# Loading the weight matrix by rows over all partitions instead of by quadrants

## The chip, the cores and the metric

The kernel runs on one core of one Trainium2 chip. The metric is the device time of one execution in microseconds (us); a time of a kernel is the median of several runs. The core has five engines that run their own instruction streams: PE (TensorE, matmul; PEld is its weight load), DVE (VectorE), ACT (ScalarE), POOL (GpSimd) and SP (SyncE, which here only issues transfers). Transfers run on the core's 16 DMA engines. SP, ACT and POOL each have a queue of their own for the transfers they issue.

## The reference

```
B, S, D = 16, 2048, 1024            # x: [B, S, D], w: [D, D], decay: [D], all float32
xw = x @ w
out[:, 0, :] = xw[:, 0, :]
for t in range(1, S):
    out[:, t, :] = decay * out[:, t - 1, :] + xw[:, t, :]
```

A matrix product, followed along time by a decayed running sum for each of the 1024 output channels.

## The kernel before

**Tiling.** Time is cut into 64 chunks of 512 steps (16 batches, 4 chunks each), and two chunks make a group. The 1024 output channels make 8 blocks of 128. A slot is one group and one block: PE sums 8 matmuls (k = 0 to 7, 128 input channels each) for each of the two chunks in PSUM, ACT, POOL and DVE run the decayed sum over it, DVE turns the result back (32x32 transposes), and SP stores it. The 1024 input channels are spread so that quadrant q of the partitions (32 partitions) holds channels 256q to 256q + 255, eight to a partition.

**The weights.** `wsb` holds w in bf16, ready for PE. It is filled from a staging area `stage[h, e]` in four quarters: h picks the left or right 512 columns, e the even or the odd rows. A quarter is 512 rows of 512 floats (1 MB). In the staging area a partition has four of them, m = 0 to 3, 512 columns each. `load_w(queues, h, e)` (L297) loads a quarter with four transfers. `settle(h, e, m, copy)` (L304, its copy is L306) casts or copies piece m of all 128 partitions into `wsb`, where it becomes the weights of k = 2m + e.

- Quarter (0, 0) is loaded at the very start, as float32, by SP and ACT in turn (the call just below `touch`). The first two transfers are SP's first and ACT's first, the others their second.
- The other three are cast to bf16 on the way by POOL's queue: (0, 1) between the first x pieces, (1, 0) and (1, 1) after the second chunk of x.

**The prologue's order is written out by hand.** The string `agenda[-99]` is carried out from left to right, and each engine keeps that order. The letters that matter: `M` loads half a chunk of x (POOL, L105, four transfers, one for each quadrant), `U` loads a w quarter on POOL's queue, `w` and `W` settle one piece on ACT or on DVE, `K` copies one element of an x quadrant into a gate (ACT, L341) and lets PE run dummy matmuls that read the gate (L324), `E` turns a piece of x (DVE, L115), `F` and `G` sort it for PE (L123).

```
-99: "M0 U0 M1 M2 M3 U1 U2 w0 W1 w2 W3 K0 K1 K2 K3 E0 E1 G0 E2 G1 E3 F2 G3 W4 w5 W6 W7 D E4 ..."
```

Ahead of it PE gets 22 dummy matmuls (`spin(22, ...)`) with nothing to wait for but a cleared tile. SP also issues four small loads of decay (L331), behind its two of w. A transfer that reuses a completion semaphore waits on its queue for the transfer that had it before; POOL has eight of them.

**The matmuls.** In slots 0 to 3 PE works through the first chunk in two pieces: for each piece first the even k (the quarter with e = 0), then the odd ones (e = 1). The right half (h = 1) is first used in slot 4. After that PE goes on slot by slot to the end, where the last four blocks are turned by PE itself and stored.

Of the kernel before, what the change touches and what calls it, by code (L numbers as in the profile page):

```python
# [14 lines left out]
def _ap(ap_obj: bass.AP, new_ap, extra_offset=0):  # L15
    return dataclasses.replace(
        ap_obj,
        ap=[list(p) for p in new_ap],
        offset=ap_obj.offset + extra_offset,
    )  # L20
# [5 lines left out]
def kernel(  # L26
# [27 lines left out]
    pin = tc.keep_in_program_order  # L54
    B, S, D = x.shape
    assert w.shape == (D, D)

    NQ = 4
    P = 32
    CQ = D // NQ  # L60
    K = CQ // P
    M = K // 2
# [4 lines left out]
    CH = D // 2  # L67
# [12 lines left out]
    def quad(q):  # L80
        return slice(q * P, (q + 1) * P)
# [184 lines left out]
    class Outlet:  # L266
# [8 lines left out]
        def store(self, b, t0):  # L275
# [4 lines left out]
            for j in range(0, self.nj, nj):  # L280
# [11 lines left out]
    stage = {(0, 0): room[0][:, 0:size],  # L292
             (0, 1): room[0][:, size:size * 3 // 2].bitcast(BF16),
             (1, 0): room[1][:, 0:size // 2].bitcast(BF16),
             (1, 1): room[1][:, size // 2:size].bitcast(BF16)}

    def load_w(queues, h, e):  # L297
        for i, q in enumerate((0, 2, 1, 3)):
            pin(queues[i % len(queues)].dma_start(  # L299
                out=stage[h, e][quad(q)].rearrange("p (m d) -> p m d", m=M),  # L300
                in_=_ap(w, [[2 * D, P], [2 * P * D, M], [1, CH]],
                        (q * CQ + e) * D + h * CH)))

    def settle(h, e, m, copy):  # L304
        src = stage[h, e][:, m * CH:(m + 1) * CH]
# [5 lines left out]
    rows = const.tile([128, 2, P], FP32, name="rows")  # L311
    touch = const.tile([128, 1], BF16, name="touch")
    load_w((nc.sync, nc.scalar), 0, 0)
    pin(nc.vector.memset(idle, 0.0))  # L314
    pin(nc.vector.memset(rows, 0.0))
# [14 lines left out]
    for q in range(NQ):  # L330
        pin(nc.sync.dma_start(  # L331
            out=rows[q * P:q * P + R],
            in_=_ap(decay, [[P, R], [CH, 2], [1, P]], q * CR)))
# [10 lines left out]
    def load_part(i):  # L344
        load_w((nc.gpsimd,), *((0, 1), (1, 0), (1, 1))[i])
# [292 lines left out]
```

## Time and profile before

| | us |
|---|---|
| median of 3 runs (904.95 to 906.10) | 905.39 |
| the profiled execution | 905.14 |
| its span, first to last instruction | 903.4 |
| time outside the span | 1.7 |
| PE busy in the span | 897.1 |
| DVE / ACT / POOL busy | 826.1 / 685.7 / 656.8 |
| first real matmul starts (L131) | 11.19 |
| first cast of w starts (L306, ACT) | 7.18 |

The span is what the profile sees of one execution; the time outside it belongs to the metric as well. Busy shares are means over the whole span. In a timeline line the first number is the start from the span's beginning, the second the length, then engine, line of the kernel, operation, output <- inputs, shape and count; several equal instructions that follow closely are one line. The bracket is the time that the engine sat idle before it, and what ended that. Where the profile lists DMA issues, the last number is the median time from issue to landing.

### The profile page before, as it was taken

How to read it: one execution, taken by the hardware profiler on the slowest of the kernel's cores; microseconds unless marked ns; L12 is line 12 of the kernel's file. 1: busy time of each engine (PE TensorE's matmuls, PEld its weight loads, DVE VectorE, ACT ScalarE, POOL GpSimd, SP SyncE). 2: the span in 40 equal slices, each digit the busy share in tenths (PEclk: the TensorE clock that was granted, in tenths of full speed). 3: DMA queues.
4: the chain of work that ended last, by engine and by line, in shares of the span. 5: the costliest groups of instructions: out<-in, count | busy, mean ns of one | idle time of the engine just before them, and what ended most of it. 6: DMA issues, size and time to landing. Idle time of an engine off the chain costs nothing.

```text
span 903.4 us, 12112 instructions
## 1 busy us (share of the span) xinstructions
PE 897.1 (99%) x4217; PEld 412.9 (46%) x4217; DVE 826.1 (91%) x628; ACT 685.7 (76%) x955; POOL 656.8 (73%) x755
## 2 busy tenths in 40 slices
PE   9999999999999999999999999999999999999997
PEld 6444444444444444444444444444444444444444
DVE  4999998999999999999998999999999999999997
ACT  4889867777877877877778778778777787787742
POOL 7988678777767768677677677777777776776632
PEclk9999999999999999999999999999999999999999
DMA  9999999999999999999999999999999999999868
GB/s 191 195 215 216 232 239 215 215 238 244 245 246 255 236 250 251 240 250 244 221 238 227 222 232 229 229 227 227 232 227 226 235 230 223 227 232 210 175 143 237
DMA packets 402542, 204.77 MB, mean 227 GB/s; under 512 B 8752, under 2 KB 401456, under 8 KB 402480
## 3 DMA queue, kind: packets, MB, share of 16 engines
q1 hardware_dynamic: 265168, 134.76, 61.0%
q0 software_dynamic: 137024, 68.70, 56.9%
q8 instruction: 33, 0.54, 0.2%
q10 hardware_dynamic: 288, 0.52, 0.2%
q14 instruction: 29, 0.24, 0.1%
HBM read 138.42 MB, written 134.22 MB: 302 GB/s over the span
## 4 chain that ended last, share of the span: by engine, by line
PE 95%; DMA 2%; POOL 1%; DVE 1%; issue 0%; ACT 0%; DVEq 0%; POOLq 0%
PE ps L131 94%; DMA xb<-in_x_dram 2%; POOL xb L105 1%; DMA ot<-in_w_dram 1%; PE spare L131 1%; DVE xw L115 0%; ACT xt L123 0%; DVE so L201 0%; DVE ot L258 0%; PE spare L388 0%; ACT xs L183 0%; PE ps L388 0%; DVE h L392 0%; ACT h L169 0%; POOL ot L299 0%
## 5 line engine op out<-in xcount | busy, mean ns | idle before, releaser
L131 PE MATMUL ps<-xt,wsb 128*128 128x512 bf16 (+2 forms) x4036 | 868.2, 378 | 0.2 <-ACT h L169 0.2
L131 PEld LDWEIGHTS <-wsb 128*128 128x128 bf16 x4168 | 407.4, 98 | 477.9 <-ACT wsb L306 0.8
L196 POOL TENSOR_TENSOR xs<-h,xs 128x512 f32<-128x512 f32 (+1 forms) x190 | 242.8, 1278 | 189.9 <-ACT h L169 85.0
L183 ACT COPY xs<-ps 128x1024 f32<-128x1024 f32 (+1 forms) x190 | 189.3, 996 | 156.2 <-PE ps L131 151.6
L258 DVE STREAM_TRANSPOSE ot<-so 128x1024 f32<-128x1024 f32 (+1 forms) x260 | 300.1, 1192 | 2.0 <-POOL so L190 1.1
L246 POOL TENSOR_TENSOR so<-h,xs 128x512 f32<-128x512 f32 (+1 forms) x190 | 241.2, 1271 | 42.6 <-ACT h L169 27.8
L123 ACT COPY xt<-xw 128x2048 bf16<-128x2048 bf16 (+3 forms) x136 | 242.2, 1790 | 7.7 <-DVE xw L115 7.7
L105 POOL DMA_DIRECT2D xb<-in_x_dram x264 | 174.2, 661 | 5.3 <-DMA xb<-in_x_dram 2.4
L169 ACT ACTIVATE h<-so,dec 128x512 f32<-128x512 f32 (+1 forms) x190 | 145.3, 766 | 27.1 <-DVE so L201 23.9
L115 DVE STREAM_TRANSPOSE xw<-xb 128x2048 f32<-128x2048 f32 (+3 forms) x78 | 147.4, 1901 | 6.3 <-DMA xb<-in_x_dram 6.3
L201 DVE TENSOR_TENSOR_SCAN so<-spare,keep,xs 128x512 f32<-128x512 f32 (+1 forms) x97 | 120.0, 1240 | 27.4 <-POOL xs L196 27.1
L201 DVE TENSOR_TENSOR_SCAN so<-spare,xs 128x512 f32<-128x512 f32 x93 | 113.3, 1220 | 27.4 <-POOL xs L196 24.5
L169 ACT ACTIVATE h<-ps,dec 128x512 f32<-128x512 f32 (+1 forms) x190 | 130.1, 685 | 0.0
L221 DVE TENSOR_TENSOR_SCAN so<-dec,ps 128x1024 f32<-128x1024 f32 x34 | 76.8, 2261 | 1.0 <-ACT h L169 1.0
L221 DVE TENSOR_TENSOR_SCAN so<-dec,keep,ps 128x1024 f32<-128x1024 f32 (+1 forms) x35 | 76.0, 2171 | 0.2 <-issue 0.2
L250 ACT COPY keep<-so 128x1 f32<-128x1 f32 x136 | 25.4, 189 | 9.5 <-DVE so L221 9.0
L192 ACT COPY so<-keep 128x1 f32<-128x1 f32 x97 | 18.5, 191 | 2.5 <-DVE ot L258 2.3
L131 PE MATMUL ps<-xw,wsb 128*128 128x256 bf16 (+3 forms) x68 | 11.2, 301 | 0.0
L190 POOL MEMSET so<- 128x1 f32 x93 | 10.7, 117 | 0.6 <-DVE ot L258 0.6
L131 PE MATMUL spare<-xt,wsb 128*128 128x512 bf16 (+3 forms) x52 | 10.7, 322 | 0.0
L324 PE MATMUL spare<-idle 128*128 128x512 bf16 x22 | 7.8, 536 | 1.2 <-DVE idle L314 1.2
L299 POOL DMA_DIRECT2D ot<-in_w_dram x12 | 6.5, 546 | 0.9 <-issue 0.4
(37 smaller groups left out, 37.2 us busy)
## 6 DMA issues: line engine op xcount, KB each, us to landing
out_dram<-ot SPq DMA_DIRECT2D x248, 512.0 KB, 10.9
xb<-in_x_dram POOLq DMA_DIRECT2D x248, 256.0 KB, 7.8
out_dram<-ot SPq DMA_DIRECT2D x12, 256.0 KB, 4.3
ot<-in_w_dram POOLq DMA_DIRECT2D x12, 128.0 KB, 5.8
xb<-in_x_dram POOLq DMA_DIRECT2D x8, 128.0 KB, 4.6
out_dram<-xb SPq DMA_DIRECT2D x3, 256.0 KB
xb<-in_x_dram POOLq DMA_DIRECT2D x4, 144.0 KB, 6.7
ot<-in_w_dram ACTq DMA_DIRECT2D x2, 256.0 KB, 5.1
```

What stands on the lines that cost most here:

```text
L105: pin(nc.gpsimd.dma_start(out=xb_of[c][quad(q), j0:j1], in_=_ap(x, [[D, P], [P * D, j1 - j0], [1, CQ]], (b * S + t0 + j0 * P) * D + q * CQ)))
L115: pin(nc.vector.transpose(out=dst.rearrange("p (m j i) -> p j m i", m=M, i=P)[:, j0:j1, m0:m1], in_=src.rearrange("p (j m c) -> p j m c", ...
L123: pin(copy(out=xt_of[c][:, m0:m1, :, j0 * P:j1 * P], in_=src))
L131: pin(nc.tensor.matmul(out=ps[:, t0:t1] if ps.shape[1] >= t1 else ps, lhsT=lhs, rhs=rhs, start=(k == 0 and t0 == start), stop=(stop and k ...
L169: pin(nc.scalar.activation(out=h, in_=src, func=mybir.ActivationFunctionType.Copy, scale=dec[:, self.n:self.n + 1]))
L183: pin(nc.scalar.copy(out=self.xs, in_=self.ps))
L196: pin(nc.gpsimd.tensor_tensor(out=odds, in0=self.g, in1=odds, op=ALU.add))
L201: pin(nc.vector.tensor_tensor_scan(out=so[:, 3:T + 2:2], data0=squares[-1][:, n:n + 1].to_broadcast([128, T // 2]), data1=self.xs[:, 1:T:2 ...
L221: pin(nc.vector.tensor_tensor_scan(out=so[:, t + 2:t + 2 + size], data0=dec[:, n:n + 1].to_broadcast([128, size]), data1=ps, initial=befor ...
L246: pin(nc.gpsimd.tensor_tensor(out=self.so[:, 2:T + 2:2], in0=self.h, in1=self.xs[:, 0:T:2], op=ALU.add))
L250: pin(nc.scalar.copy(out=self.keep, in_=self.so[:, self.T + 1:self.T + 2]))
L258: pin(nc.vector.transpose(out=outlet.ot[:, :, c0:c0 + P], in_=self.so[:, 2 + t0:2 + t0 + nj * P].rearrange("p (i t) -> p i t", t=P)))
```

## The change

Only `load_w` changes. Before, transfer i of a quarter fills one quadrant: 32 partitions, each with its four rows m = 0 to 3. After, transfer m fills one piece: row m of every one of the 128 partitions, in the columns m·512 to m·512 + 511 of the staging area. The bytes, the number of transfers, the queues and the place of the issues stay. The source pattern of a transfer was [32 partitions, 4 rows, 512 columns] and becomes [4 quadrants, 32 partitions, 512 columns]; the destination was 32 x 4 x 512 and becomes 128 x 512.

```diff
     def load_w(queues, h, e):
-        for i, q in enumerate((0, 2, 1, 3)):
-            pin(queues[i % len(queues)].dma_start(
-                out=stage[h, e][quad(q)].rearrange("p (m d) -> p m d", m=M),
-                in_=_ap(w, [[2 * D, P], [2 * P * D, M], [1, CH]],
-                        (q * CQ + e) * D + h * CH)))
+        for m in range(M):
+            pin(queues[m % len(queues)].dma_start(
+                out=stage[h, e][:, m * CH:(m + 1) * CH],
+                in_=_ap(w, [[CQ * D, NQ], [2 * D, P], [1, CH]],
+                        (2 * P * m + e) * D + h * CH)))
```

With it the waits change: before, a settle waited for all four transfers of its quarter, since each brings a part of every piece; after, a settle of piece m waits for transfer m alone. The order of the instructions on PE, DVE, ACT, POOL and SP is the same in both kernels. In the first quarter SP has m = 0 and 2, ACT has m = 1 and 3; of the settles, ACT has m = 0 and 2, DVE m = 1 and 3.

## The prediction

> **What bounds the kernel now.** I read the page first, then the timeline of the first 42 us, then the table of one-microsecond stretches, then the list of DMA issues, and last the end of the trace.
>
> ```profile
> span 903.4 us, 12112 instructions
> ...
> PE 897.1 (99%) x4217; PEld 412.9 (46%) x4217; DVE 826.1 (91%) x628; ACT 685.7 (76%) x955; POOL 656.8 (73%) x755
> ...
> PE 95%; DMA 2%; POOL 1%; DVE 1%; issue 0%; ACT 0%; DVEq 0%; POOLq 0%
> ```
>
> PE is busy for all but 6.3 us of the span, and 95% of the chain that ends last is PE. What happens once the first real matmul runs can hardly be shortened; a later first matmul moves everything behind it. The w loads stand only in the prologue, so the timeline of the prologue decides (start, duration, engine; in brackets the idle time before and what ended it):
>
> ```profile
> 0.74 0.90 ACTq L299 DMA_DIRECT2D ot<-in_w_dram  x2
> 0.75 0.86 SPq L299 DMA_DIRECT2D ot<-in_w_dram  x2
> ...
> 1.20 7.78 PE L324 MATMUL spare<-idle 128*128 128x512 bf16 x22 [1.20 <-DVE idle L314]
> ...
> 7.18 1.14 ACT L306 CAST wsb<-ot 128x512 bf16<-128x512 f32 x2 [4.02 <-DMA ot<-in_w_dram]
> ...
> 8.23 0.19 ACT L341 COPY gate<-xb 32x1 bf16<-32x1 bf16 x1
> ...
> 8.82 2.54 PE L324 MATMUL spare<-idle,gate 128*128 128x512 bf16 x11
> ...
> 11.19 0.55 PE L131 MATMUL ps<-xw,wsb 128*128 128x288 bf16 x3
> ```
>
> PE is never idle from 1.20 on: 22 dummy matmuls, then 11 that wait for the gate copies, then real work at 11.19. ACT makes the gate copies (K0 to K3 of the agenda) only after w0 and w2, its two casts of the first w quarter, and those wait 4.02 us for the loads. So a late w load holds up ACT, ACT the gates, and the gates PE. DVE likewise has W1 and W3 ahead of E0, the first transpose of x.
>
> **Step 1: how many DMA engines carry a load.** Bytes, number of loads (4 per quarter) and pieces (128 rows of 2 KB) stay the same. What changes is the shape. Before, both sides of a load begin with a dimension of 32. Changed, the source begins with 4 (the quadrants), the destination with 128 (the partitions). The kernel has one other load that begins with 4: decay.
>
> ```profile
> ot<-in_w_dram ACTq DMA_DIRECT2D x2, 256.0 KB, 5.1
> ot<-in_w_dram SPq DMA_DIRECT2D x2, 256.0 KB, 4.8
> ...
> rows<-in_decay_dram SPq DMA_DIRECT2D x4, 1.0 KB
> ```
>
> The w loads have a landing time behind their size, decay has none: this view gives one only when it finds sixteen completions for each transfer. In the trace's semaphore updates a w load counts sixteen while its data lands; the first decay load counts one at its issue, at 2.15, and four later. So a transfer that begins with 4 seems to be carried by four engines. The bounds for the new loads are 16 engines and 4; I take 4, the row that it is nearest to.
>
> [...]
>
> **Step 2: when the first quarter lands.** The stretches (PE, PEld, DVE, ACT, POOL busy, then clock, DMA share, GB/s):
>
> ```profile
> 2.00:3.00 1.00, 1.00 (x4) 0.42 (x3) 0.00 (x0) 0.99 (x2) 1.00 (x3) 1.00 0.91 258
> 3.00:4.00 1.00, 1.00 (x4) 0.33 (x3) 0.00 (x0) 0.16 (x1) 1.00 (x3) 1.00 0.98 332
> ...
> 12.00:13.00 1.00, 1.00 (x10) 0.75 (x9) 0.79 (x4) 1.00 (x2) 1.00 (x3) 1.00 1.45 194
> ```
>
> From 3 to 4 us only SP's and ACT's loads run: 332 GB/s over 16 engines is 20.8 GB/s each, 99 ns for a row of 2,048 B. The best slices in the DMA view of the first 3 us, 410 GB/s, give 80 ns. The quarter has 512 rows: 32 for each of 16 engines, but 128 for each of four. That is 10.2 us at 80 ns and 12.6 at 99; I take 89 ns, 11.4 us.
>
> Beside them come the first x pieces, issued by POOL from 1.31 to 3.86, spread over all engines: 4 x 144 KB, 590 KB, at the 194 GB/s of the third line 3.0 us of every engine's time. How the queues share an engine no row shows; bounds 0 and 3.0, and I take two thirds, 2.0, since two w queues stand against one of x.
>
> Data flows from 2.0 on. By 3.8 the 524 KB of the first two loads have been started (6 KB in the stretch before, 258, and 0.78 of 332), and the later one lands at 5.0 (0.74 + 4.3), so landing adds up to 1.2, the slowest engine included; I take 1.0 and 0.5 as the low end. The last transfers of the quarter land at 2.0 + 11.4 + 2.0 + 1.0 = **16.4 us** (bounds 12.7 and 18.8), where now the casts start at 7.18. The 4 x loads share the same four engines and are all in at about 17.4 instead of 10.1.
>
> **Step 3: what that does to PE.** Each cast now waits for one load instead of four, but that buys nothing: w0 and W1 go early, and w2 and W3 stand behind the late pair. At 16.4 w2 takes 0.6 (two in 1.14). From the first gate copy to the first gated matmul it takes 0.4 now (8.23 to the weight load at 8.60). So PE goes on at 17.4. Its 22 dummies end at 8.98: it idles for 8.4 us. What the clock does then stands at the end of the trace:
>
> ```profile
> 898.22 0.27 PE L388 MATMUL spare<-ident,so 128*128 128x128 f32 x1
> ```
>
> ```profile
> 900.00:902.00 2.00, 0.00 (x0) 0.00 (x0) 0.00 (x0) 0.00 (x0) 0.00 (x0) 0.83 0.79 299
> 902.00:903.40 1.40, 0.00 (x0) 0.00 (x0) 0.00 (x0) 0.00 (x0) 0.00 (x0) 0.50 0.00 1
> ```
>
> The last matmul ends at 898.5. A mean clock of 0.83 over 900 to 902 is 1.0 for 1.3 us and 0.5 after, so it fell at 901.3, 2.8 us after PE stopped. An idle time of 8.4 us is three times that. The slow pace is in the prologue too: the first dummies' weight loads start 0.43 apart until 6.72, and the last seven fit in 1.39. So the 11 gated dummies take 11 x 0.43 = 4.7 us, not 2.4 (8.82 to 11.19). The last two of them wait for K3 at about 17.4 + 0.6, well within that. The first real matmul starts at 17.4 + 4.7 = 22.1, which is **10.9 us** later than 11.19. How long the slow clock lasts: 5.9 us in the prologue (1.20 to 7.1), which would slow 1.2 us of real work too, +0.6; if it lasts only half as long, five or six dummies run fast and 1.2 come back. I count 0.
>
> Does a load come later still? The four engines have (128 - 32) x 89 ns = 8.5 us more to do than now, and all x loads wait for them. The DMA share stays above 1 (1.45 in the third line above), so there is no slack to catch up in, and every later x and w transfer is about 8.5 us late, with PE 10.9 late: 2.4 us of cover. Without the clock's part (2.3) it would be 8.6 against 8.5, so the loss would still be that. Nothing gives it back, as PE works without a gap from 11.19 to the tail.
>
> **Step 4: the other three quarters.** POOL issues 12 loads of 128 KB at 0.54 each; that stays. If each uses four engines but the next load the next four, four in flight fill all 16: nothing. If all use the same four: 131 KB at 194 GB/s is 0.68 us over 16 engines and 2.7 over four, so 12 x 2.0 = 24 us more there. No row shows which; I take nothing, because POOL's loads are issued in fours, and keep the other end as a rival. [...]
>
> **Sum.** Profiled execution 905.14 us (span 903.4 and 1.7 around it) + 10.9 = 916.0. The median of the three runs, 905.39, is 0.25 above the profiled one: **916.3 us**. By the bounds of step 2 it is 7 to 13.5 us of loss, 912 to 919.
>
> **Rivals.**
> 1. The loads keep all 16 engines. For it: they reach all 128 partitions, and the decay row is of tiny transfers. Then the loads cost what they do now. Were they faster, PE's dummies would still run to 11.19. 905.4 us, not slower; it decides when the SP and ACT loads land at 7 us or before. Chance 0.06.
> 2. PE's clock stays up, or the rows go at 80 ns or better: 8.6 us late, by the x and w transfers or the 2.4 us of dummies. 914 us. Against it: 8.4 us of idle time. Chance 0.10.
> 3. The four engines hinder each other, as each walks through one quadrant of partitions in step: a row takes half as long again, 133 ns, 17.0 us for the quarter. Landing at 22.6, first matmul 28.3, +17. 922 us. Chance 0.12.
> 4. POOL's loads all stay on four engines: the last quarters come 8.5 + 24 us late, and now the weights of the second half are cast at 26.3 to 28.4 with PE waiting 0.2 to 0.4 for them. About 936 us. Chance 0.06.
>
> [...]
>
> **How the numbers follow.** The forecast has 0.64, and 0.02 is left for something unforeseen, which I put on the faster side. The range 912 to 924 takes in the forecast with its bounds and rivals 2 and 3, 0.86 less their tails. 0.2% is 1.8 us, about what the measurement can tell from no change: faster 0.02, same 0.06 (rival 1), slower 0.92.
>
> **What would show it.** Step 1: SP's and ACT's w loads lose their landing time in the list of issues, and the stretch 3 to 4 us moves some 80 to 100 GB/s at a DMA share near 0.25. Step 2: the casts of w2 and W3 start near 16.4. Step 3: PE idles about 8 us from 9.0, the gated dummies come 0.43 apart, and the first matmul of L131 starts near 22. Step 4: PE has no new gaps from there to 42 us. I am wrong if SP's and ACT's loads land by 7, if PE waits for L306 or L123 after its start, or if the loss lies outside the first 42 us.

## The result, and the profile after

The changed kernel takes **919.62 us** (median; 919.05 to 920.47) against 905.49 for the kernel before beside it: a ratio of 1.0155, 95% interval 1.0143 to 1.0167. It is slower by 14.1 us, inside the range of 912 to 924 and 3.3 us above the forecast of 916.3. Its profiled execution took 919.15 us. The page of its profile, span, engines and chain:

```profile
span 917.4 us, 12101 instructions
...
PE 898.1 (98%) x4217; PEld 413.2 (45%) x4217; DVE 827.1 (90%) x628; ACT 686.1 (75%) x955; POOL 658.1 (72%) x755
...
PEclk7999999999999999999999999999999999999999
...
PE 93%; DMA 3%; POOL 2%; ACT 1%; issue 0%; DVE 0%; POOLq 0%
```

PE is busy 1.0 us longer, the span is 14.0 longer: the loss is time in which PE waits, not work. The one slice (22.9 us) in which the granted clock is lower is the first. The timeline of after's prologue (start, duration, engine; in brackets the idle time before and what ended it):

```profile
0.74 1.72 ACTq L299 DMA_DIRECT2D ot<-in_w_dram  x2
0.75 1.47 SPq L299 DMA_DIRECT2D ot<-in_w_dram  x2
...
1.20 7.04 PE L324 MATMUL spare<-idle 128*128 128x512 bf16 x22 [1.20 <-DVE idle L314]
...
9.07 0.43 DVE L306 CAST wsb<-ot 128x512 bf16<-128x512 f32 x1 [7.56 <-DMA ot<-in_w_dram]
...
13.82 0.62 ACT L306 CAST wsb<-ot 128x512 bf16<-128x512 f32 x1 [9.84 <-DMA ot<-in_w_dram]
16.49 0.43 DVE L306 CAST wsb<-ot 128x512 bf16<-128x512 f32 x1 [7.00 <-DMA ot<-in_w_dram]
...
19.11 0.62 ACT L306 CAST wsb<-ot 128x512 bf16<-128x512 f32 x1 [4.68 <-DMA ot<-in_w_dram]
...
19.64 0.83 ACT L341 COPY gate<-xb 32x1 bf16<-32x1 bf16 x4
...
19.88 3.87 PE L324 MATMUL spare<-idle,gate 128*128 128x512 bf16 x11 [11.64 <-ACT gate L341]
...
23.59 0.54 PE L131 MATMUL ps<-xw,wsb 128*128 128x288 bf16 x3
```

The reader is to see the chain that was forecast: each cast ends a long wait for its load, the last at 19.11 instead of 7.18; the gates follow at 19.64; PE has then been idle for 11.64 us; and the first real matmul starts at 23.59 instead of 11.19, **12.4 us later**. The list of DMA issues of after (operation, count, KB each, and, where it is found, the median landing time):

```profile
ot<-in_w_dram ACTq DMA_DIRECT2D x2, 256.0 KB
ot<-in_w_dram SPq DMA_DIRECT2D x2, 256.0 KB
...
rows<-in_decay_dram SPq DMA_DIRECT2D x4, 1.0 KB
```

SP's and ACT's w loads have lost their landing time, as decay had none before; in the semaphore updates each counts one at its issue and four later (ACT's first at 2.11, then 8.22 to 9.04; before it counted sixteen, 4.25 to 5.01). The stretches (PE, PEld, DVE, ACT, POOL busy, then clock, DMA share, GB/s) say the same, and show the clock:

```profile
2.00:3.00 1.00, 1.00 (x4) 0.42 (x3) 0.00 (x0) 0.51 (x1) 1.00 (x3) 1.00 0.21 43
3.00:4.00 1.00, 1.00 (x4) 0.33 (x3) 0.00 (x0) 0.96 (x2) 1.00 (x3) 1.00 0.31 69
...
8.00:9.00 1.00, 0.24 (x2) 0.00 (x0) 0.00 (x0) 0.00 (x0) 0.00 (x0) 1.00 1.44 147
...
12.00:13.00 1.00, 0.00 (x0) 0.00 (x0) 0.00 (x0) 0.00 (x0) 0.00 (x0) 0.68 0.33 93
...
16.00:17.00 1.00, 0.00 (x0) 0.00 (x0) 0.43 (x1) 0.00 (x0) 0.07 (x1) 0.50 0.29 80
...
22.00:23.00 1.00, 1.00 (x5) 0.45 (x4) 0.47 (x3) 0.89 (x2) 0.41 (x1) 0.70 0.94 106
```

Where 332 GB/s ran from 3 to 4 us, 69 run now, at a DMA share of about 0.3 (four engines of 16 are 0.25). Up to 18 us the share is high, 0.95 to 1.44, only from 4 to 11, when POOL's first eight transfers run beside; from 12 to 14 and from 16 to 18 us it is near 0.3 again. The clock's mean of 0.68 over 12 to 13 puts its fall near 12.4, 0.70 over 22 to 23 its rise near 22.6.

The rest of the loss is in what PE waits for in the first 60 us of after (total, times, longest):

```profile
PE spare L324 <- ACT gate L341: 11.6, 1, 11.6
...
PE ps L131 <- ACT xt L123: 0.8, 1, 0.8
PE ps L131 <- ACT h L169: 0.5, 1, 0.5
```

The last two are 1.3 us. Before has only one such wait in that time:

```profile
PE ps L131 <- ACT h L169: 0.2, 1, 0.2
```

So of 14.0 us of span, 12.4 are the later start, 1.1 are additional waits near 54 us, and 0.5 are not placed. What POOL waits for shows why loads come late a second time. Before, and then after:

```profile
POOL xb L105 <- DMA xb<-in_x_dram: 2.4, 2, 2.0
```

```profile
POOL xb L105 <- DMA xb<-in_x_dram: 11.9, 4, 6.5
```

POOL's transfers take turns on eight completion semaphores in both traces, so eight may be under way, here four of x and four of w. Its first x load frees a place only when it lands (12.8 us instead of 7.8, the fourth 20.0 instead of 10.1), and the loads of the next half chunk of x are issued only then (from 13.04 to 20.29 instead of 8.07 to 10.39). Each of the eight has twelve of its sixteen completions by 12.7 us and waits for the last four, so most engines have nothing to do while the DMA share is 0.3.

### The profile page after: what moved, and what is told of

Read it like the earlier page. It is cut to its first block, busy times and chain, and to the rows that moved or that the text cites. A ratio compares the mean times of both kernels' runs of the same rounds, so it can differ in the third digit from the quotient of the medians.

```text
span 917.4 us, 12101 instructions
## 1 busy us (share of the span) xinstructions
PE 898.1 (98%) x4217; PEld 413.2 (45%) x4217; DVE 827.1 (90%) x628; ACT 686.1 (75%) x955; POOL 658.1 (72%) x755
## 4 chain that ended last, share of the span: by engine, by line
PE 93%; DMA 3%; POOL 2%; ACT 1%; issue 0%; DVE 0%; POOLq 0%
PE ps L131 93%; DMA ot<-in_w_dram 3%; POOL xb L105 1%; PE spare L131 1%; ACT xt L123 0%; POOL ot L299 0%; POOL xs L196 0%; POOL so L246 0%; ACT h L169 0%; PE spare L388 0%; ACT xs L183 0%; PE ps L388 0%; DVE h L392 0%; POOL so L190 0%; POOLq L196 0%
## 5 line engine op out<-in xcount | busy, mean ns | idle before, releaser
L201 DVE TENSOR_TENSOR_SCAN so<-spare,keep,xs 128x512 f32<-128x512 f32 (+1 forms) x97 | 120.0, 1240 | 27.5 <-POOL xs L196 27.2
L324 PE MATMUL spare<-idle,gate 128*128 128x512 bf16 x11 | 3.9, 524 | 11.6 <-ACT gate L341 11.6
```

The source lines that it names most:

```text
L201: pin(nc.vector.tensor_tensor_scan(out=so[:, 3:T + 2:2], data0=squares[-1][:, n:n + 1].to_broadcast([128, T // 2]), data1=self.xs[:, 1:T:2 ...
```

## The experiments

**The theory** put to the test: a load whose source begins with 4 is carried by four DMA engines; the late first quarter is nearly the whole loss, and the other three quarters cost little. **The rivals:** the shape of the piece costs, not the number of engines; the engines hinder each other; the clock's fall is what costs; POOL's loads cost as well. All ratios are to the kernel before, run beside each (905.1 to 905.3 us).

**1. The first quarter alone by rows.**

```diff
-        load_w((nc.gpsimd,), *((0, 1), (1, 0), (1, 1))[i])
+        load_w_quads((nc.gpsimd,), *((0, 1), (1, 0), (1, 1))[i])
```

(`load_w` is the changed one, `load_w_quads` the one before.)

> Only the first quarter (SP and ACT) is loaded by rows; POOL's twelve transfers are as before. Theory (four engines carry the first quarter): nearly the whole loss stays, 917 to 920 us, with the first real matmul of L131 near 23 us. Rival (POOL's three quarters, also on fewer engines, make a good part of the loss): 910 to 914 us.

Measured: 917.92 us, 1.0140 (1.0126 to 1.0153). What PE waits for in its first 60 us:

```profile
PE spare L331 <- ACT gate L348: 10.9, 1, 10.9
```

Its timeline has the dummies behind the gates:

```profile
19.93 4.66 PE L331 MATMUL spare<-idle,gate 128*128 128x512 bf16 x11 [10.87 <-ACT gate L348]
24.43 0.55 PE L131 MATMUL ps<-xw,wsb 128*128 128x288 bf16 x3
```

The first real matmul starts at 24.43, 13.2 later than before, and beside the 1.2 us at the very start, which before has too, the list has no further wait. The first quarter alone makes 12.7 of the 14.1 us.

**2. The other three quarters alone by rows** (POOL's twelve loads; the edit is the opposite one, at L313).

> Only POOL's three quarters are loaded by rows; the first quarter is as before. Theory: POOL's transfers take the four next engines in turn, so 904.5 to 907 us, and the first real matmul stays near 11.2 us. Rival (POOL's transfers all use the same four engines): 925 us or more; half of the loss here would be 912 us.

Measured: 910.85 us, 1.0065 (1.0051 to 1.0079). Missed: these loads are not free, they cost 5.6 us by themselves. What PE waits for, and a stretch of five microseconds:

```profile
PE ps L131 <- DVE xw L115: 1.6, 2, 0.9
PE ps L131 <- ACT xt L123: 1.5, 2, 0.8
...
PE spare L331 <- ACT gate L348: 0.7, 1, 0.7
PE ps L131 <- ACT h L169: 0.5, 1, 0.5
```

```profile
25.00:30.00 5.00, 4.95 (x37) 3.55 (x38) 4.57 (x9) 4.96 (x9) 3.39 (x8) 1.00 1.28 149
```

The same stretch before:

```profile
25.00:30.00 5.00, 5.00 (x27) 2.35 (x26) 4.89 (x4) 4.08 (x10) 4.89 (x8) 1.00 1.44 195
```

The four waits are 4.3 us, where before has 0.2, and the span is 5.1 longer; the gate's 0.7 is in the start of the first real matmul, 0.8 later (11.99), and the others come behind it, up to 46.5 us. From 10 to 30 us the DMA engines are about as busy as before (a share of 1.31; before, 1.24 to 1.44) but bring 153 GB/s instead of 192 to 198. The last w load lands at 30.6 instead of 25.9. Two things on the page of e2 and in its timeline differ: its issues last 0.67 to 0.70 us instead of 0.54, and its packets are more:

```profile
DMA packets 407150, 204.78 MB, mean 225 GB/s; under 512 B 13360, under 2 KB 406064, under 8 KB 407088
```

13,360 packets under 512 B instead of 8,752 are 4,608 more. The packet records (the trace's list of every DMA packet) have them in POOL's queue, 4 bytes each: 384 for each of twelve loads, which would be 32 for each of twelve engines, if four carry a load's rows.

**3. The first quarter in sixteen transfers**, one row of one quadrant each.

```diff
-    load_w((nc.sync, nc.scalar), 0, 0)
+    load_w_pieces((nc.sync, nc.scalar), 0, 0)
...
+        for m in range(M):
+            for q in (0, 2, 1, 3):
+                pin(queues[m % len(queues)].dma_start(
+                    out=stage[h, e][quad(q), m * CH:(m + 1) * CH],
+                    in_=_ap(w, [[2 * D, P], [1, CH]],
+                            (q * CQ + 2 * P * m + e) * D + h * CH)))
```

> The first quarter comes piece by piece, as in the change, but each piece in four transfers of one quadrant (32 partitions, 64 KB), whose patterns begin with 32; POOL as before. Theory (the number of engines is what costs): 16 engines again, 904.5 to 908 us, the first quarter in by 8 us. Rival (that a piece for all partitions must land before a cast, or the order by pieces, is what costs): 914 us or more.

Measured: 910.87 us, 1.0065 (1.0052 to 1.0077). Missed, and the experiment was badly made: SP's and ACT's issues stretch over 5.9 and 6.1 us instead of 0.9, since with sixteen the later ones wait for a semaphore of an earlier one; what ACT does next was released by a w load, at 6.87. The first real matmul came at 16.85, 5.66 later, which is the whole loss of 5.6. On the shape of the pieces it says nothing; run 10 repeats it without that flaw.

**4. Two engines:** the first quarter in eight transfers, one row over 64 partitions each, the source beginning with 2.

```diff
+        for m in range(M):
+            for q in (0, 2):
+                pin(queues[m % len(queues)].dma_start(
+                    out=stage[h, e][q * P:(q + 2) * P, m * CH:(m + 1) * CH],
+                    in_=_ap(w, [[CQ * D, 2], [2 * D, P], [1, CH]],
+                            (q * CQ + 2 * P * m + e) * D + h * CH)))
```

> The first quarter by rows, but each row in two transfers of two quadrants, so that the source pattern begins with 2; POOL as before. Theory (the first dimension sets the number of engines): two engines have 256 rows each instead of 128, some 10.5 us more at 83 ns a row, so about 930 us and the last cast of w near 30 us. Rival (the loss is that of 128-partition transfers, whatever the engines): 915 to 921 us, as with the change.

Measured: 932.24 us, 1.0298 (1.0284 to 1.0312). Its timeline:

```profile
33.25 4.87 PE L332 MATMUL spare<-idle,gate 128*128 128x512 bf16 x11 [25.57 <-ACT gate L349]
...
37.92 0.84 PE L131 MATMUL ps<-xw,wsb 128*128 128x288 bf16 x3
```

The last cast is at 32.48 instead of 19.11. Half the first dimension brings the quarter in 1.7 times as late, and the loss follows.

**5. The same four transfers with a source that begins with 128.** It uses one stride over all partitions; other rows of w then stand on each partition (neighbouring partitions read rows 8 apart instead of 2), so that x meets other weights than in the reference.

```diff
-                in_=_ap(w, [[CQ * D, NQ], [2 * D, P], [1, CH]],
-                        (2 * P * m + e) * D + h * CH)))
+                in_=_ap(w, [[K * D, 128], [1, CH]],
+                        (2 * m + e) * D + h * CH)))
```

> The changed kernel with one difference: partition p takes row 8p + 2m + e of w, so that the source pattern is [128 partitions, 512 columns] instead of [4, 32, 512] (the weights then stand in other partitions, and the product is another one). Transfers, bytes, 128 partitions, 2 KB rows, queues and waits are those of the change. Theory (the first dimension of 4 puts a load on four engines): 16 engines again, 904 to 907 us, first matmul of L131 at 11.2 us, and POOL's three quarters cost nothing either. Rival (loads that reach all 128 partitions, or that bring one piece each, are what costs): 912 us or more.

Measured: 905.82 us, 1.0008 (0.9999 to 1.0017). Its timeline:

```profile
5.40 0.62 ACT L306 CAST wsb<-ot 128x512 bf16<-128x512 f32 x1 [0.45 <-DMA ot<-in_w_dram]
...
5.72 0.43 DVE L306 CAST wsb<-ot 128x512 bf16<-128x512 f32 x1 [0.79 <-DMA ot<-in_w_dram]
...
11.37 0.55 PE L131 MATMUL ps<-xw,wsb 128*128 128x288 bf16 x3
```

One row on all 128 partitions, in one transfer, is no handicap at all: the quarter is in at 5.7, 1.3 us before that of the kernel before. Its page has no additional small packets (8,752). Both parts of the loss, the late quarter and POOL's, go when the first dimension goes from 4 to 128. That w comes earlier gains nothing, because the dummies and the x loads (the gates wait for them until 10.7) hold the first matmul.

**6. A longer warm-up:** after with 75 free dummies instead of 22, which keep the clock up.

```diff
-    spin(22, idle[:, 0:128])
+    spin(75, idle[:, 0:128])
```

> The changed kernel with 75 dummy matmuls instead of 22, so that PE works until the gates open. If PE's start alone sets the end: the 11 gated dummies take 2.4 us instead of 3.9, the first matmul of L131 comes near 22.2, and the time falls by 1.4 us, to about 918.2. If the late x loads set it, as PE's two waits near 53 us in the changed kernel suggest: the earlier start is given back there, 919.2 to 920.

Measured: 920.98 us, 1.0169 (1.0156 to 1.0183); the profiled execution took 919.61. Its timeline:

```profile
19.81 2.54 PE L324 MATMUL spare<-idle,gate 128*128 128x512 bf16 x11
22.18 0.55 PE L131 MATMUL ps<-xw,wsb 128*128 128x288 bf16 x3
...
52.56 1.02 PE L131 MATMUL ps<-xt,wsb 128*128 128x512 bf16 x4 [1.40 <-ACT xt L123]
...
54.36 1.02 PE L131 MATMUL ps<-xt,wsb 128*128 128x512 bf16 x4 [0.78 <-ACT xt L123]
...
55.86 1.89 PE L131 MATMUL ps<-xt,wsb 128*128 128x512 bf16 x8 [0.48 <-ACT h L169]
```

The clock stays at 1.0 and real work starts 1.4 us earlier than in after, but PE then waits 2.8 us instead of 1.3. The earlier start is given back whole: with the clock up, what PE needs of x comes no earlier than in after, so the late x sets the end. The clock's fall has no price of its own there.

**7. The first quarter with nothing beside it:** after, but POOL's loads wait for the whole quarter (a single run).

```diff
+    held = const.tile([128, M], FP32, name="held")
+    pin(nc.gpsimd.tensor_tensor(out=held, in0=stage[0, 0][:, 0:size:CH],
+                                in1=stage[0, 0][:, 1:size:CH], op=ALU.add))
```

> The changed kernel, but POOL's first load waits until the first quarter is in (POOL reads it first), so that four engines carry the first quarter with nothing beside. Theory (83 to 89 ns a row on each engine, sharing with x made the rest): 128 rows from 2.2 us are in by 13 to 14.5 us, against 19.1. Rival (the four engines hinder each other, 133 ns a row): 19 us or later.

Measured: 920.96 us. Its timeline, the last two casts:

```profile
12.43 0.43 DVE L306 CAST wsb<-ot 128x512 bf16<-128x512 f32 x1 [5.27 <-DMA ot<-in_w_dram]
13.48 0.62 ACT L306 CAST wsb<-ot 128x512 bf16<-128x512 f32 x1 [3.46 <-DMA ot<-in_w_dram]
```

The packet records have its rows from 2.19 to 13.24: 11.05 us for 128 rows on each of four engines, 86 ns a row, within the 80 to 99 ns that the prediction read with 16 engines at work. So these four engines hinder each other by little or nothing; the 133 ns of rival 3 are out. In after, the same cast starts at 19.11, so sharing the engines with what POOL has issued, x above all, costs 5.6 us.

**8. Longer issues:** before, with two small memsets behind each of POOL's w loads, 0.2 us each time.

```diff
+            if queues[0] is nc.gpsimd:
+                for _ in range(2):
+                    pin(nc.gpsimd.memset(blank, 0.0))
```

> The kernel before, with two small memsets behind each of POOL's twelve loads of w, so that an issue takes POOL 0.2 us longer, which is more than the 0.14 by which the new shape lengthens it. If the longer issue makes the 5.6 us that POOL's three quarters cost alone: 909 us or more. If it is the transfers themselves: 905 to 906.5 us.

Measured: 907.19 us, 1.0020 (1.0011 to 1.0029), 0.7 us above what was expected. 0.2 us more on each issue costs 1.9 us, so e2's 0.13 to 0.16 may be some 1.4 of its 5.6, if the cost is in proportion.

**9. POOL's loads on two engines each:** before with POOL's twelve loads as 24, by the function of run 4.

> Before, with only POOL's twelve quarter loads by rows, each split into two halves of 64 partitions (a first dimension of two), 24 transfers instead of 12. Theory A (what costs is the 4-byte pieces that a load by rows puts on the engines that carry none of its rows): 24 transfers with 32 x 14 pieces each are 10,752 more of them in POOL's queue instead of e2's 4,608, the engines' share of data falls below e2's 149 to 157 GB/s between 10 and 30 us, and the time is 913 to 918. Theory B (what costs is that one engine reads a whole row of 128 pieces by itself): two engines carry each transfer just as badly, few more small pieces appear, and the time is about e2's, 910 to 912. The issues double in number as well; e8 priced 0.2 us more on each of 12 issues at 1.9 us, so up to some 2 to 4 us of any loss can be theirs.

Measured: 918.57 us, 1.0142 (1.0125 to 1.0158), 13.4 us of loss. That is 0.6 above theory A's range, far from theory B's, and nearly in proportion to the additional pieces (5.6 us for 4,608, 13.4 for the 10,752 that were expected). But the issues had doubled too, and that had to be taken out (run 11).

**10. The first quarter in eight transfers of two rows over one quadrant**, each with a source that begins with 32, as in the kernel before, where a load counts sixteen completions.

```diff
+        for m in range(0, M, 2):
+            for i, q in enumerate((0, 2, 1, 3)):
+                pin(queues[i % len(queues)].dma_start(
+                    out=stage[h, e][quad(q), m * CH:(m + 2) * CH].rearrange(
+                        "p (m d) -> p m d", m=2),
+                    in_=_ap(w, [[2 * D, P], [2 * P * D, 2], [1, CH]],
+                            (q * CQ + 2 * P * m + e) * D + h * CH)))
```

> Before, with only the first quarter in eight transfers of two rows over one quadrant of 32 partitions (instead of two of which each brings four rows to 32 partitions, four in all), so that 16 engines still carry each. Theory (the number of engines decides, not the shape of the piece): first matmul within 0.7 us of before's 11.19, time 905 to 907. Rival (any further splitting of the quarter delays it, as e3's 16 transfers did): first matmul above 13, time 908 to 911.

Measured: 906.28 us, 1.0014 (1.0005 to 1.0022). Its timeline:

```profile
9.71 2.55 PE L333 MATMUL spare<-idle,gate 128*128 128x512 bf16 x11 [1.21 <-ACT gate L350]
12.09 0.55 PE L131 MATMUL ps<-xw,wsb 128*128 128x288 bf16 x3
```

The time is as expected, the first matmul 0.9 later instead of at most 0.7. So eight transfers on 16 engines cost 1.1 us, where eight on two engines (run 4) cost 27. The number of transfers, the bytes and the queues are the same in both; the number of engines makes the difference.

**11. POOL's loads as 24 transfers on 16 engines:** the function of run 10 for POOL's quarters.

> Before, with only POOL's twelve quarter loads split in two, two rows over one quadrant each: 24 transfers as in e9, but each with a first dimension of 32, so 16 engines carry it. It takes the number of issues out of e9's loss. Theory A (e9's and e2's loss comes from the 4-byte pieces of transfers that few engines carry): no additional 4-byte pieces but those of 12 more completions (192), data at 180 GB/s or more between 25 and 40 us, and 905.5 to 909, where e8's price of longer issues is in. Rival (the doubled number of issues made e9's loss beyond e2's): 910.5 to 914 here.

Measured: 912.61 us, 1.0082 (1.0065 to 1.0099). The rival held: twice as many transfers cost 7.4 us with no engine left out (8,944 small packets, 192 more, the sixteen completions of each of twelve more loads). The same stretch of e11, and what POOL does in it:

```profile
25.00:30.00 5.00, 5.00 (x43) 4.01 (x42) 4.09 (x9) 4.27 (x8) 4.77 (x9) 1.00 0.73 105
```

```profile
25.23 4.31 POOL L307 DMA_DIRECT2D ot<-in_w_dram  x8 [0.53 <-DMA ot<-in_w_dram]
```

Here the engines are idle more (0.73; before 1.44), and POOL sets the pace: it issues eight loads one behind the other, 0.54 us each, and each brings half the bytes that such an issue brought before. Up to 20 us it also waits for a free place among its eight, 4.1 us for x. How the 7.4 us divide between the two is open. Run 9, and then run 11, ten microseconds later:

```profile
35.00:40.00 5.00, 2.62 (x6) 0.54 (x7) 3.29 (x4) 2.14 (x6) 4.17 (x9) 0.52 1.15 115
```

```profile
35.00:40.00 5.00, 5.00 (x25) 2.29 (x24) 3.52 (x4) 2.22 (x5) 4.75 (x7) 1.00 1.44 193
```

Run 9 takes 6.0 us more than run 11 (918.57 - 912.61). That is near the 5.6 that four engines cost in run 2, but it is not the price of the two engines alone. From 11 us on PE waits 7.9 us in run 9 and 5.5 in run 11, and it is busy for 902.6 us instead of 899.0: its clock, which fell near 18 us in both, fell a second time in run 9 (0.52). So loads that come late cost twice there, the wait itself and the slow clock after it, and the proportion that run 9 seemed to show does not hold.

## Why the prediction was right, and where its terms were off

Times of the profiled executions; predicted, then measured:

| step | predicted | measured | difference |
|---|---|---|---|
| last cast of the first quarter starts | 16.4 | 19.11 | +2.7 |
| first x loads all in | 17.4 | 20.0 | +2.6 |
| PE resumes | 17.4 | 19.88 | +2.5 |
| from there to the first real matmul | 4.7 | 3.7 | -1.0 |
| first real matmul | 22.1 | 23.59 | +1.5 |
| PE's additional waits after it | 0 | 1.1 | +1.1 |
| whole execution | 916.0 | 919.15 | +3.1 |

2.5 - 1.0 + 1.1 are 2.6 of the 3.1; 0.5 is not placed. The direction and the path were right. Three terms were off, and that two of them partly cancelled was luck.

**Step 1, four engines: right.** The issue list, four completions a load, 69 GB/s, and runs 4, 5 and 10 show it; rival 1 (all 16 engines) is out. The prediction took it from the decay row, an estimate; in the runs of the first quarter, sources that begin with 2, 4 and 128 gave 932.2, 917.9 to 919.6 and 905.8 us, and in the semaphore updates their loads have 2, 4 and 16 completions as data lands (runs 4, after and 5). A load of before, whose source begins with 32, has 16 as well. What other first dimensions would give was not shown.

**Step 2, the quarter's landing: the mechanism was right, one term was mis-sized.** The rows alone were 11.4 us, measured 11.05 (run 7), so rival 3 (133 ns a row, an assumption that no run shows) is out. (By its own terms, 2.0 + 17.0 + 2.0 + 1.0, its quarter lands at 22.0 and not at 22.6; that changes its 922 us by half a microsecond.) The share with x was 2.0, with a bound of 3.0, and measured 5.6. The bound was the fault. It took x's bytes at the 194 GB/s of a stretch in which the share of 1.45 counts packets that overlap on an engine. The four x loads are 1,152 pieces of 512 B, 72 for each engine, and a piece takes 60 ns (median of the packet records): if they ran one after the other that alone were 4.3 us, an estimate. What the records show of the 5.6 us is that a row of w took 110 ns in the mean, against 87 in run 7, which is 3.0 us for the 128 rows of an engine; the rest is time in which the engine had no such row under way. Why the rows themselves take longer beside x is open. 19.1 also lies just above the bound of 18.8.

**Step 3, the clock: right, and its size a matter of luck.** It fell, and gated dummies ran at half pace (0.43 us apart at a granted clock of 0.50): 3.7 us instead of the 4.7 that was taken. The other case that was named gives 3.5 (4.7 less 1.2); by its own figures it is 3.8, since half of 5.9 us holds seven dummies at 0.43, and the other four save 0.9. In run 1, with the last cast at the same time (19.16), all eleven ran slow and it was 4.5 (19.93 to 24.43). The clock rose 2.7 us after PE resumed in after and 4.3 in run 1, and nothing in the prediction tells which it will be. Rival 2 (the clock stays up, 914 us) is out: it fell, and run 6, where longer dummies keep it up, takes 920.98 us.

**Step 3's last part failed:** "every later x and w transfer is about 8.5 us late", with 2.4 us of cover. The last w load lands at 39.1 instead of 25.9, the first x load of the next chunk at 40.6 instead of 27.5: 13 us late, with PE 12.4 late. There was no cover. The reason given, a DMA share above 1 all along, was read from the kernel before; after, the share is near 0.3 from 12 to 14 and from 16 to 18 us, because POOL's eight places are held by transfers that still wait for their part on the four slow engines.

**Step 4, the other quarters cost nothing: wrong by itself.** POOL's loads do not all use the same four engines: in after, of the 512 rows of its first quarter, 384 were read by 12.2 us and 128, as many as one load has, only from 18.8 on, when the last row of the late quarter had started (18.5), and run 2 takes 910.85 us where its expectation had 925 or more for the same four. So rival 4 (all on the same four) is out. That fits loads that take other engines in turn, as the author had assumed. Yet such loads cost 5.6 us alone (run 2). In the changed kernel, beside the late first quarter, they cost 1.7 (919.62 - 917.92), which the sum lacked; even that is no clean price, as the first real matmul of run 1 came 0.8 later than that of after, by the clock. Longer issues are at most some 1.4 of the 5.6 by run 8. Whether the rest is in the 4-byte pieces or in the uneven load of the engines stays **open**: 4,608 pieces of 9 ns (the median in the records) over 16 engines would be 2.6 us, and 10,752 would be 6.0, an estimate, but runs 2, 9 and 11 don't separate them from the unevenness that comes with them. The packet records of run 2 say only that the pieces' own time is not all: from 10 to 30 us they hold 0.14 of the share of 1.31 (before, 0.03 of 1.37), while a piece of x took 70 ns in the mean instead of 60, and a row of w 109 instead of 98.

## What to carry to other kernels

Look at the first dimension of a transfer's source before anything else: here 2 or 4 ahead of the first quarter's bytes made 27 and 13 us, and 128 ahead of all four quarters 0.5. When a transfer that leads a prologue gets slower, count also the places that a queue has for transfers under way, since what they hold back is late a second time, while engines stand idle. Price shared engines by packets and their duration, not by a mean rate, and take a proportion out of two runs as a finding only when a third holds the other difference fixed.

## What was unexpected in the hardware

- In the new shape each load of POOL's queue has 4-byte pieces besides, 384 a load; with twelve such loads the data rate from 10 to 30 us fell from between 192 and 198 to 153 GB/s at the same busy share (run 2).
- Such a load still counts sixteen completions, not four: in after the first of them has twelve at 8.8 to 10.5 us and the last four at 21.7 to 22.3, when the late quarter is through.
- SP's first w row started at 4.48 us in after (1.84 before), ACT's at 2.18 (2.44 before): on four engines SP's queue began behind ACT's, and in run 7, without x, still only at 3.95.
- The issue of a load takes longer in the new shape: two take 1.47 us on SP and 1.72 on ACT instead of 0.86 and 0.90, and one takes 0.7 instead of 0.54 on POOL.
- The clock fell 4.1 us after PE stopped (8.24 to 12.4), where the end of the kernel before showed 2.8, and rose 2.7 us after PE resumed (19.88 to 22.6), in run 1 4.3 (19.93 to 24.2). The stretch at half clock lasted 10.24 us in after (12.35 to 22.59), some 10.2 in run 1, 27.3 in run 4 and 3.4 in run 11; what sets these lengths and delays was not shown.
